# Memory keys and values moved behind the projection units, unit ends cut into steps, the last two units interleaved

## The chip, the cores and the metric

One Trainium2 chip, and one of its cores. The metric is the device time of one launch in microseconds (us); a profiled execution also has a span, from its first instruction to its last. TensorE (PE) multiplies matrices; VectorE (DVE) and ScalarE (ACT) work element by element and empty the accumulators; GpSimd (POOL) does masks and small powers and issues stores; SyncE (SP) issues the loads. Each engine takes its instructions strictly in the order in which they are written for it, so whatever stands behind an instruction that waits, waits too.

## The reference

One layer of a trunk with three parallel mixers, 1024 tokens, width 1024, in float32:

```python
h = rms_norm(x, g_mix[l])
proj = h @ w_in[l]
c_h, c_b, c_c, sq, sk, sv, xq, gate_pre = jnp.split(proj, split_idx, axis=-1)
y_conv = (c_b * causal_depthwise_conv(c_c * c_h, conv_w[l])) @ w_conv_out[l]
o_sb = stick_breaking_attention(to_heads(sq), to_heads(sk), to_heads(sv))
y_sb = o_sb.transpose(0, 2, 1, 3).reshape(b, s, SB_DIM) @ w_sb_out[l]
mem_n = rms_norm(mem, g_mem[l])
y_x = memory_cross_attention(xq, mem_n, w_mem_kv[l], q_norm_g[l], k_norm_g[l]) @ w_x_out[l]
...
merged = gates[:, :, 0] * y_conv + gates[:, :, 1] * y_sb + gates[:, :, 2] * y_x
x = x + merged @ w_out[l]
h2 = rms_norm(x, g_mlp[l])
x = x + jnp.square(jax.nn.relu(h2 @ w_up[l])) @ w_down[l]
```

`mem` has 256 rows; its keys and values are `mem_n @ w_mem_kv` (1024 by 2048), and the keys are normed per head of 256.

## The kernel before

Every float32 operand is split into a high part (ACT casts it to fp32r) and a low part (DVE subtracts), and a product is three matmuls: high by high, high by low, low by high. Stages follow each other:

1. **First stage.** `kv(cg)` makes 256 columns of the memory's keys (`cg` 0 to 3) or values (4 to 7): 2 row tiles of 24 matmuls of 256 columns, in the accumulator `z`. Weights come by `kv_load` (two loads of 512 KB) and are split by `kv_split`. `norm_transpose` turns the normed memory rows into `mem_t`. Keys and values are stored in `kv_scr` and read again later.
   Most of the projections of `h` go through a `Unit`: two blocks of 128 columns for all 1024 tokens by seven products instead of eight (`p1`, `p2`, `p6`, `p5`, `p7`, `p3`, `p4`), each of 12 matmuls of 512 columns; so 84 matmuls a unit. `w1` to `w4` prepare the weights, one `w` for each pair of products, two pairs ahead. `Seconds.first` transposes the first 512 tokens before the first unit; `second_a` and `second_b` make the sums with the other 512 and are called from `hooks` between products. There are 13 units: four for the memory queries (`QUnit`), and three times `HUnit`, `CUnit`, `BUnit` for the convolution. `drive` writes them out pair by pair. `fin` ends a unit; that of a `CUnit` multiplies two tiles, scales each on ACT and adds two shifted copies of each on DVE (`taps`). The calls of `vec`, `act`, `split_o` are pinned to this order (`keep_in_program_order`); the other instructions are put in order by the scheduler.
2. **Heads' values.** `v_steps`: 16 groups of 24 matmuls of 512 columns, which need four weight tiles `us` (split with `unit`, L89 and L90) and `hx`; `h12`, a part of `hx`, is loaded again from `h12_scr` and split first.
3. Cross attention over the memory (`x_scores`, `x_values`), woven with projections; then the stick-breaking attention of 8 pairs of heads, woven with projections (`more`).
4. **Output matrices.** Three times eight blocks (`w_co`, `w_so`, `w_xo`) with the gates, then `w_out` with the residual in `acc`; each finished row tile is normed and stored in `x_scr`.
5. **The wide matrix.** 16 `FUnit`s of the same seven products; `post` and `direct` apply relu and square, `fin` makes sums and stores seven parts in `f_scr`.
6. **The way back.** 28 parts `n` of 48 matmuls (`fetch` loads, `prep` splits), each added to a half of four `acc` tiles on DVE. `acc` is read again from `x_scr` on POOL's queue.

Order in `drive` for the ends and the last pair:

```python
            second()
            if done:
                done.fin()
                done = None
            hook(n, 1)
```

Four buffers of 512 KB (`rawp`) take the loads, three (`whlp`) the split weights, and 40 pages of 512 KB (`pgp`) nearly everything else.

Of the kernel before, what the change touches and what calls it, by code (L numbers as in the profile page):

```python
# [16 lines left out]
P = 128  # L17
# [25 lines left out]
def block_kernel(ctx, tc, x, mem, small, w_in, w_v, w_kv, w_co, w_so, w_xo, w_out, w_up, w_dn, out):  # L43
# [137 lines left out]
    def run(gen):  # L181
        for _ in gen:
            pass

# [149 lines left out]
    class Unit:  # L334
# [86 lines left out]
        def fin(self):  # L421
            pass

    def drive(U, hooks, late=None):

        NU = len(U)
        pairs = [(1, u) for u in range(4)] + [(2, 0), (2, 1), (3, 0), (3, 1)]
        for u in range(2, NU):  # L430
            pairs += [(k, u) for k in ((1, 2, 3) if u >= 4 else (2, 3))]

        def prep(n):
            if n < len(pairs):
                k, u = pairs[n]
                getattr(U[u], f"w{k}")()

        def hook(n, i):
            hooks.get((n, i), lambda: None)()

        for u in range(4):
            U[u].r1 = load(U[u].s1_)
        for n in range(2):
            prep(n)
        hook(-1, 0)
        U[3].bank = po
        done = None
        for n, (k, u) in enumerate(pairs):
            un = U[u]
            first, second = ((un.p1, un.p2), (un.p6, un.p5), (un.p7, un.p3))[k - 1]  # L450
            final = n == len(pairs) - 1
            if final and late:
                late(0)
            first()
            prep(n + 2)
            if n == 1:
                U[0].load()
            if n + 1 < len(pairs) and pairs[n + 1][0] == 3:
                v = pairs[n + 1][1]
                U[v].w4()  # L460
                if v + 2 < NU:
                    U[v + 2].load()
            hook(n, 0)
            if n == 2:
                U[1].load()
            if final and late:
                late(1)
            second()
            if done:
                done.fin()  # L470
                done = None
            hook(n, 1)
            if k == 3:
                if final and late:
                    late(2)
                un.p4()
                done = un
        done.fin()
# [4 lines left out]
    kv_scr = [[dram.tile([P, 1024], F32, name=f"kvscr_{n}_{i}") for i in range(NM)] for n in range(2)]  # L483
# [15 lines left out]
    def kv(cg):  # L499

        us = kv_w.pop(cg)
        to = kn if cg < 4 else vr
        for i in range(NM):
# [10 lines left out]
            nc.scalar.copy(to[i][:, c0 : c0 + 256], ps)  # L514

    def k_norm(i):
# [14 lines left out]
        nc.gpsimd.dma_start(out=kv_scr[0][i], in_=kn[i])  # L531

    mrows = load_rows(mem, 0, NM)
    kv_load(0)
    kv_load(1)
    xrows = load_rows(x, 0, 4)
    mts = [normed(t) for t in mrows]
    mnt = [(page(), page()) for _ in range(2)]
    mem_t = [cut(mnt[k // 4], (k % 4) * M, (k % 4 + 1) * M) for k in range(KT)]
    kv_split(0)  # L540
    run(norm_transpose(mts, lambda k: mem_t[k], C_GMEM))
    kv_split(1)
    kv_load(2)
    kn = [page(F32) for _ in range(NM)]
    run(kv(0))
    rows0 = [normed(t) for t in xrows]
    kv_load(3)
    run(kv(1))
    xrows = load_rows(x, 512, 4)
    kv_split(2)  # L550
    weave(sec_h.first(rows0), kv(2))
    kv_split(3)
    kv_load(4)
    rows1 = [normed(t) for t in xrows]
    run(kv(3))
    for i in range(NM):
        k_norm(i)
    del kn
    vr = [page(F32) for _ in range(NM)]
    kv_split(4)  # L560
    run(kv(4))

    def kv_late(cg):
        kv_split(cg)
        if cg + 1 < 8:
            kv_load(cg + 1)
        run(kv(cg))
        if cg == 7:
            for i in range(NM):
                nc.gpsimd.dma_start(out=kv_scr[1][i], in_=vr[i])  # L570
            pin[0] = False


    class QUnit(Unit):
# [13 lines left out]
    def taps(c, prod, cv, act, stt):  # L588

        act(cv, prod, AF.Copy, scale=tap(c, 2))  # L590
        for j in (1, 2):
            stt(
                out=cv[:, j:1024],
                in0=prod[:, 0 : 1024 - j],
                scalar=tap(c, 2 - j),
                in1=cv[:, j:1024],
                op0=ALU.mult,
                op1=ALU.add,
            )
# [5 lines left out]
    class CUnit(Unit):  # L605
# [6 lines left out]
        def fin(self):  # L612
            self.cv = []
            for i in range(2):
                prod = flat(self.tiles[i])
                vec(prod, prod, ALU.mult, flat(self.hu.tiles[i]))
                cv = flat(self.hu.tiles[i])
                taps(self.c0 + i, prod, cv, act, lambda **kw: order(nc.vector.scalar_tensor_tensor(**kw)))
                self.cv.append(cv)
            self.tiles = self.hu.tiles = None  # L620
# [19 lines left out]
    def a_(kk, cg=None):  # L640
        def go():
            sec_h.second_a(rows1, kk)
            if cg:
                kv_late(cg)

        return go
# [668 lines left out]
```

## Time and profile before

| | us |
|---|---|
| median of 3 runs (2278.94 to 2281.53) | 2281.45 |
| the profiled execution, its own time | 2278.89 |
| its span | 2277.2 |
| PE busy, 10148 instructions | 2180.7 (96%) |
| DVE busy | 1405.6 (62%) |
| ACT busy | 1004.0 (44%) |
| POOL busy | 384.1 (17%) |
| mean granted TensorE clock, share of full | 0.981 |

PE is busy nearly all the time, so the time that is not matmul at full clock is what there is to look for: stretches in which PE is idle, and stretches with a lower granted clock. A view of windows gives both for any stretch: the length, PE's busy time, and the granted clock (`PEclk`). Of two matmuls in a row in the timeline the difference of the starts is the time that one costs; the duration beside it includes pipeline overlap.

### The profile page before, as it was taken

To read this page: it belongs to the slowest core of one execution; us is meant where nothing else is said; L and a number is where in the kernel's file an instruction comes from. 1 tells how busy PE (TensorE), PEld (TensorE's weight loads), DVE (VectorE), ACT (ScalarE), POOL (GpSimd) and SP (SyncE) were. 2 spreads that over 40 slices of the span, in tenths; PEclk is the share of its full clock that TensorE was granted. 3 is DMA by queue.
4 is the path that set the end of the run, shared out by engine and by line. 5 is a ranking of instruction groups with operands and counts; after the bars stand their busy time and mean duration, and the time that the engine had idled before them with its cause. 6 is when DMAs were issued, how large, how long until landed. Compare 5 with 4: busy or idle time off the path is not lost.

```text
span 2277.2 us, 27042 instructions
## 1 busy us (share of the span) xinstructions
PE 2180.7 (96%) x10148; PEld 1804.3 (79%) x10148; DVE 1405.6 (62%) x1885; ACT 1004.0 (44%) x1791; POOL 384.1 (17%) x570
## 2 busy tenths in 40 slices
PE   6799998999999999999999999999989999899999
PEld 6678777888878778778778788888768888688887
DVE  5454555135687788788787534442475555577776
ACT  7333324235566566565566312121465555433332
POOL 1000000112333333433333000000111111100000
PEclk9899999999999999999999999999999999999999
DMA  5332224233222222222222445333234444743443
GB/s 213 120 126 97 71 68 157 86 109 112 77 72 75 84 74 66 83 75 68 81 84 71 137 144 162 107 102 148 105 119 162 152 153 152 257 168 133 153 148 139
DMA packets 76035, 268.13 MB, mean 118 GB/s; under 512 B 9856, under 2 KB 9856, under 8 KB 75904
## 3 DMA queue, kind: packets, MB, share of 16 engines
q1 hardware_dynamic: 54400, 192.47, 26.3%
q0 software_dynamic: 21504, 73.94, 8.6%
q8 instruction: 80, 1.31, 0.2%
q14 instruction: 51, 0.42, 0.1%
HBM read 184.05 MB, written 73.92 MB: 113 GB/s over the span
## 4 chain that ended last, share of the span: by engine, by line
PE 57%; issue 20%; DVE 9%; POOL 7%; ACT 6%; DMA 1%; POOLq 0%; DVEq 0%; ACTq 0%; SPq 0%
PE d L204 5%; PE d L203 5%; PE d L205 5%; PE d L125 4%; PE d L126 4%; PE d L127 4%; PE d L281 4%; PE d L277 4%; PE d L280 4%; POOL pg L866 3%; PE z L281 2%; PE z L277 2%; PE z L280 2%; DVE pg L114 2%; POOL fscr_s L1163 1%
## 5 line engine op out<-in xcount | busy, mean ns | idle before, releaser
L203 PE MATMUL d<-pg,whl 128*128 128x512 f32 x736 | 294.5, 400 | 0.3 <-ACT ox L774 0.3
L236 ACT ACTIVATE pg<-pg 128x512 f32<-128x512 f32 (+1 forms) x192 | 150.7, 790 | 313.2 <-DVE pg L233 311.0
L204 PE MATMUL d<-pg,whl 128*128 128x512 f32 x736 | 287.8, 391 | 0.0
L205 PE MATMUL d<-pg,whl 128*128 128x512 f32 x736 | 287.8, 391 | 0.0
L866 POOL TENSOR_SCALAR_AFFINE_SELECT pg<-pg 128x128 f32<-128x128 f32 x256 | 170.0, 670 | 280.8 <-ACT pg L863 269.7
L876 DVE TENSOR_TENSOR_SCAN pg<-pg,zero 128x128 f32<-128x128 f32 (+7 forms) x128 | 177.0, 1383 | 57.0 <-POOL pg L866 54.2
L233 DVE TENSOR_TENSOR pg<-pg,pg 128x1024 fp32r<-128x1024 f32 (+3 forms) x180 | 183.8, 1031 | 44.8 <-ACT pg L236 42.5
L113 ACT CAST pg<-t 128x256 fp32r<-128x256 f32 (+2 forms) x336 | 115.2, 368 | 203.3 <-DVE pg L114 144.0
L277 PE MATMUL d<-pg,whl 128*128 128x512 f32 x420 | 168.7, 402 | 17.5 <-ACT pg L236 13.8
L280 PE MATMUL d<-pg,whl 128*128 128x512 f32 x420 | 168.0, 400 | 3.3 <-DVE pg L233 3.2
L281 PE MATMUL d<-pg,whl 128*128 128x512 f32 x420 | 167.5, 399 | 1.2 <-DVE whl L233 1.0
L205 PEld LDWEIGHTS d<-pg,whl 128*128 128x128 f32 x736 | 138.1, 188 | 30.7
L203 PEld LDWEIGHTS d<-pg,whl 128*128 128x128 f32 x736 | 138.4, 188 | 25.7 <-ACT ox L774 1.1
L204 PEld LDWEIGHTS d<-pg,whl 128*128 128x128 f32 x736 | 138.6, 188 | 24.3
L277 PE MATMUL z<-pg,whl 128*128 128x512 f32 x396 | 155.9, 394 | 0.0
L280 PE MATMUL z<-pg,whl 128*128 128x512 f32 x396 | 155.2, 392 | 0.0
L281 PE MATMUL z<-pg,whl 128*128 128x512 f32 x396 | 155.0, 391 | 0.0
L125 PE MATMUL d<-pg,whl 128*128 128x512 f32 x384 | 150.6, 392 | 3.2 <-ACT whl L89 3.2
L89 ACT CAST whl<-raw 128x1024 fp32r<-128x1024 f32 x78 | 82.5, 1057 | 159.5 <-DMA raw<-in_w_co 53.1
L126 PE MATMUL d<-pg,whl 128*128 128x512 f32 x384 | 150.3, 392 | 0.0
L233 DVE TENSOR_TENSOR whl<-pg,whl 128x1024 fp32r<-128x1024 f32 x58 | 71.1, 1226 | 127.9 <-ACT whl L236 127.9
L127 PE MATMUL d<-pg,whl 128*128 128x512 f32 x384 | 149.9, 391 | 0.0
(200 smaller groups left out, 4859.0 us busy)
## 6 DMA issues: line engine op xcount, KB each, us to landing
raw<-in_w_in SPq DMA_DIRECT2D x76, 512.0 KB, 3.6
raw<-in_w_up SPq DMA_DIRECT2D x36, 512.0 KB, 3.6
raw<-fscr_s SPq DMA_DIRECT2D x32, 512.0 KB, 3.6
pg<-in_w_dn SPq DMA_DIRECT2D x32, 512.0 KB, 4.9
gscr<-pg POOLq DMA_DIRECT2D x24, 512.0 KB, 2.9
raw<-gscr SPq DMA_DIRECT2D x24, 512.0 KB, 3.7
fscr<-pg POOLq DMA_DIRECT2D x48, 256.0 KB, 2.8
fscr_s<-pg POOLq DMA_DIRECT2D x48, 256.0 KB, 2.8
```

Source lines behind the costliest of these rows:

```text
L125: nc.tensor.matmul(ps, lhsT=ah, rhs=bh, start=i == 0, stop=False)
L126: nc.tensor.matmul(ps, lhsT=ah, rhs=bl, start=False, stop=False)
L127: nc.tensor.matmul(ps, lhsT=al, rhs=bh, start=False, stop=i == n - 1)
L203: nc.tensor.matmul(ps, lhsT=ah, rhs=bh, start=i == 0, stop=False)
L204: nc.tensor.matmul(ps, lhsT=ah, rhs=bl, start=False, stop=False)
L205: nc.tensor.matmul(ps, lhsT=al, rhs=bh, start=False, stop=i == n - 1)
L233: order(nc.vector.tensor_tensor(out=out, in0=a, in1=b, op=op))
L277: m_ = nc.tensor.matmul(ps, lhsT=ah, rhs=bh, start=first and i == 0, stop=False, **go)
L280: nc.tensor.matmul(ps, lhsT=ah, rhs=bl, start=False, stop=False, **go)
L281: nc.tensor.matmul(ps, lhsT=al, rhs=bh, start=False, stop=i == n - 1, **go)
L866: nc.gpsimd.affine_select(out=t_[:, W - P : W], in_=t_[:, W - P : W], pattern=[[-1, P]], compare_op=ALU.is_gt, fill=fill_, base=0, channel ...
L876: nc.vector.tensor_tensor_scan(out=rev, data0=rev, data1=zero.broadcast_to([P, W]), initial=1.0, op0=ALU.mult, op1=ALU.add)
```

## The change

- The memory's keys and values leave the first stage. It now begins with the first 512 tokens' norms and transposes, and the units follow. `mem`'s loads, norms, transposes, the eight `kv(cg)`, and `k_norm` stand in the stage of the heads' values, woven with `v_steps`: each `kv(cg)` with two of its half groups. `kv_scr` is gone; the values are split straight from the accumulator into `vx`.
- `drive` becomes a class `Drive`: `start` loads and splits the first weights, `run` writes the rest. A unit's `fin` is a generator, and one step of the oldest unfinished one is written at each hook. `CUnit.fin` is now four steps: both multiplications, both scalings, then the shifts of one tile and of the other. `FUnit.fin` has two.
- The last two units are written pair by pair side by side, so the last `CUnit` and the last `BUnit`, and the last two `FUnit`s, end together.
- `Drive.start` of the `FUnit`s stands before the last row tiles of `w_out`; `w_co`'s first tile is loaded (`w_first`) before the rest of `more`.
- `acc` is read back in quarters of 128 by 512 for each group of four tiles, two of the four groups before the last `FUnit` products and two after; `block`, `fetch` and `prep` of the first part stand one to four pairs earlier.

```diff
-    def drive(U, hooks, late=None):
...
-        for u in range(2, NU):
-            pairs += [(k, u) for k in ((1, 2, 3) if u >= 4 else (2, 3))]
+    class Drive:
...
+            for u in range(2, NU - 2):
+                self.pairs += [(k, u) for k in ((1, 2, 3) if u >= 4 else (2, 3))]
+            self.pairs += [(k, u) for k in (1, 2, 3) for u in (NU - 2, NU - 1)]
...
+            def hook(n, i):
+                hooks.get((n, i), lambda: None)()
+                if late:
+                    late(n - NP, i)
+                if ends:
+                    if next(ends[0], 0) == 0:
+                        ends.pop(0)
...
+                if k == 3:
+                    un.p4()
+                    ends.append(un.fin())
+            for e in ends:
+                run(e)
...
+            if cg < 4:
+                nc.scalar.copy(kn[i][:, c0 : c0 + 256], ps)
+            else:
+                split(ps, vx[i][0][:, c0 : c0 + 256], vx[i][1][:, c0 : c0 + 256])
...
         def fin(self):
...
+            for i in range(2):
+                vec(prod[i], prod[i], ALU.mult, self.cv[i])
+            yield 1
+            for i in range(2):
+                act(self.cv[i], prod[i], AF.Copy, scale=tap(self.c0 + i, 2))
+            yield 1
+            for i in range(2):
+                for j in (1, 2):
+                    shift(self.c0 + i, j, prod[i], self.cv[i], lambda **kw: order(nc.vector.scalar_tensor_tensor(**kw)))
+                yield 1
...
+    xrows = load_rows(x, 0, 4)
+    dr = Drive(units)
+    rows0 = [normed(t) for t in xrows]
+    dr.start()
+    xrows = load_rows(x, 512, 4)
+    run(sec_h.first(rows0))
+    rows1 = [normed(t) for t in xrows]
+    dr.run(weaving(sec_h, rows1))
...
-    fill(vgen, 17)
+    fill(vgen, 2)
+    mts = [normed(t) for t in load_rows(mem, 0, NM)]
+    kv_load(0)
...
+    for _ in norm_transpose(mts, lambda k: mem_t[k], C_GMEM):
+        fill(vgen, 1)
...
+    for cg in range(8):
+        if cg + 1 < 8:
+            kv_load(cg + 1)
+        if cg == 4:
+            for i in range(NM):
+                k_norm(i)
+            vx[:] = [(page(), page()) for _ in range(NM)]
+        weave(kv(cg), vgen_n(vgen, 2))
+        if cg + 1 < 8:
+            kv_split(cg + 1)
...
+    w_first = unit(w_co[0])
     run(more)
...
+            if ch == 1 and t == 6:
+                df.start()
...
+        elif (n, i) == (-2, 1):
+            prep(0, 0)
+            for t in range(8):
+                acc[t] = page(F32)
+            reload(0, 0)
+        elif (n, i) == (-1, 0):
+            prep(0, 1)
+            reload(4, 1)
...
+    df.run(weaving(sec_f, rows[4:8]), ahead)
+    reload(0, 1)
+    reload(4, 0)
```

PE at the start of the program, before: transposes of the memory rows (tiles `t`) and the keys' matmuls into `z`.

```order
L176 MATMUL t_169<-ident,pg_143 128x128
L176 MATMUL t_174<-ident,pg_143 128x128
L176 MATMUL t_169<-ident,pg_151 128x128
L176 MATMUL t_174<-ident,pg_151 128x128
L203 MATMUL z_222<-whl_162,pg_158 128x256
L204 MATMUL z_222<-whl_162,pg_158 128x256
```

The same place after the change; `pg_127` to `pg_151` are the first four normed row tiles of `x`, `d_279` and `z_297` the first two products of the first unit, `pg_248` a row tile of the other 512 tokens.

```order
L302 MATMUL t_180<-ident,pg_127 128x128
L302 MATMUL t_186<-ident,pg_127 128x128
L302 MATMUL t_180<-ident,pg_135 128x128
...
L284 MATMUL d_279<-pg_192,whl_166 128x512
L287 MATMUL d_279<-pg_193,whl_166 128x512
...
L284 MATMUL z_297<-pg_192,whl_166 128x512
...
L302 MATMUL t_315<-ident,pg_248 128x128
...
L284 MATMUL d_335<-pg_192,whl_168 128x512
```

The units' products have moved to the front; no keys stand before or among them.

DVE at the end of the first stage, before (L618 are the shifts of the last `CUnit`, which stand well before the last products; `pg_2574` and `pg_2521` the last `BUnit`, `raw_2606` the reloaded `h12`, `raw_2672` the first weights of the heads' values).

```order
L618 SCALAR_TENSOR_TENSOR pg_2337<-pg_2453,sm,pg_2337 128x1022
L233 TENSOR_TENSOR pg_2545<-raw_2308,pg_2545 128x512
L233 TENSOR_TENSOR pg_2574<-d_2487,pg_2543 128x512
L233 TENSOR_TENSOR pg_2521<-z_2547,pg_2543 128x512
L233 TENSOR_TENSOR pg_2521<-pg_2521,pg_2281 128x1024
L233 TENSOR_TENSOR pg_2574<-pg_2574,pg_2337 128x1024
L233 TENSOR_TENSOR pg_2615<-raw_2606,pg_2614 128x512 x2
L233 TENSOR_TENSOR pg_2620<-raw_2608,pg_2619 128x512 x2
L90 TENSOR_TENSOR pg_2675<-raw_2672,pg_2674 128x1024
```

And after it (L596 are those shifts, `z_1888` the last product but one, `raw_2060` the first weights of the heads' values):

```order
L240 TENSOR_TENSOR pg_1830<-z_1888,pg_1878 128x512
L596 SCALAR_TENSOR_TENSOR pg_1675<-pg_1794,sm,pg_1675 128x1023
L596 SCALAR_TENSOR_TENSOR pg_1675<-pg_1794,sm,pg_1675 128x1022
L596 SCALAR_TENSOR_TENSOR pg_1729<-pg_1915,sm,pg_1729 128x1023
L596 SCALAR_TENSOR_TENSOR pg_1729<-pg_1915,sm,pg_1729 128x1022
L240 TENSOR_TENSOR pg_1830<-pg_1830,pg_1675 128x1024
L240 TENSOR_TENSOR pg_1958<-pg_1958,pg_1729 128x1024
L240 TENSOR_TENSOR pg_2003<-raw_1998,pg_2002 128x512 x2
L240 TENSOR_TENSOR pg_2008<-raw_2000,pg_2007 128x512 x2
L90 TENSOR_TENSOR pg_2063<-raw_2060,pg_2062 128x1024
```

The four shifts now stand between the last product but one and the first split of the next stage.

DVE where the way back begins, before (`pg_15861`, `pg_15863` are `acc` tiles, `pg_15901` and `pg_15936` the weights' differences for part 1):

```order
L233 TENSOR_TENSOR xh_15858<-pg_15800,pg_15848 128x512
L233 TENSOR_TENSOR pg_15901<-pg_15784,pg_15772 128x1024
L233 TENSOR_TENSOR pg_15904<-pg_15901,pg_15903 128x1024
L233 TENSOR_TENSOR pg_15861<-d_15885,pg_15861 128x512
L233 TENSOR_TENSOR whl_15906<-raw_15780,whl_15906 128x1024
L233 TENSOR_TENSOR pg_15863<-d_15886,pg_15863 128x512
L233 TENSOR_TENSOR pg_15936<-pg_15786,pg_15774 128x1024
```

After (`pg_15800` is the last split of part 0, `z_15686` the last unit's product, `pg_15895` and `pg_15930` the differences for part 1, `pg_15753` an `acc` tile):

```order
L240 TENSOR_TENSOR pg_15800<-raw_15703,pg_15799 128x1024
L240 TENSOR_TENSOR pg_15622<-z_15686,pg_15676 128x512
L240 TENSOR_TENSOR pg_15577<-pg_15577 128x512
L240 TENSOR_TENSOR xh_15833<-pg_15717,pg_15807 128x512
L240 TENSOR_TENSOR pg_15850<-pg_15622,pg_15792 128x512
L240 TENSOR_TENSOR pg_15850<-pg_15850,pg_15622 128x512
L240 TENSOR_TENSOR pg_15622<-pg_15622 128x512
L240 TENSOR_TENSOR xh_15860<-pg_15792,pg_15850 128x512
L240 TENSOR_TENSOR pg_15895<-pg_15727,pg_15645 128x1024
L240 TENSOR_TENSOR pg_15898<-pg_15895,pg_15897 128x1024
L240 TENSOR_TENSOR pg_15753<-d_15879,pg_15753 128x512
L240 TENSOR_TENSOR whl_15900<-raw_15723,whl_15900 128x1024
```

The sums of two units now stand between the splits of part 0 and the differences of part 1; the additions into `acc` keep their place behind these.

More of the change, by code (lines that the diff above doesn't have):

```diff
@@ L183, in run, with vgen_n @@
             pass
+    def vgen_n(gen, n):
+        for _ in range(n):
+            if next(gen, 0) == 0:
+                return
+            yield 1
     def chain(*gens):
@@ new lines, in fin, with __init__, prep, start @@
+            yield 1
+    class Drive:
+        def __init__(self, U):
+            self.U = U
+            NU = len(U)
+            self.pairs = [(1, u) for u in range(4)] + [(2, 0), (2, 1), (3, 0), (3, 1)]
+            for u in range(2, NU - 2):
+                self.pairs += [(k, u) for k in ((1, 2, 3) if u >= 4 else (2, 3))]
+            self.pairs += [(k, u) for k in (1, 2, 3) for u in (NU - 2, NU - 1)]
+        def prep(self, n):
+            if n < len(self.pairs):
+                k, u = self.pairs[n]
+                getattr(self.U[u], f"w{k}")()
+        def start(self):
+            for u in range(4):
+                self.U[u].r1 = load(self.U[u].s1_)
+            for n in range(2):
+                self.prep(n)
+        def run(self, hooks, late=None):
+            U, pairs = self.U, self.pairs
+            NU, NP = len(U), len(pairs)
+            ends = []
+            def hook(n, i):
[5 more added lines that the diff above has]
+                        ends.pop(0)
+            U[3].bank = po
+            for n, (k, u) in enumerate(pairs):
+                un = U[u]
+                first, second = ((un.p1, un.p2), (un.p6, un.p5), (un.p7, un.p3))[k - 1]
+                first()
+                self.prep(n + 2)
+                if n == 1:
+                    U[0].load()
+                if n + 1 < NP and pairs[n + 1][0] == 3:
+                    v = pairs[n + 1][1]
+                    U[v].w4()
+                    if v + 2 < NU:
+                        U[v + 2].load()
+                hook(n, 0)
+                if n == 2:
+                    U[1].load()
+                second()
+                hook(n, 1)
+                if k == 3:
[3 more added lines that the diff above has]
+                run(e)
@@ L530, in k_norm @@
             )
[L531 to L571, printed above, removed]
     class QUnit(Unit):
@@ L1072, in block_kernel @@
             g = load(g_scr[b][d])
-            w = unit(wsrc[d])
+            w = w_first if b + d == 0 else unit(wsrc[d])
             for th in range(2):
@@ L1097, in block_kernel, with __init__, post, direct @@
     }
+    class FUnit(Unit):
+        def __init__(self, u):
+            super().__init__(w_up[u], w_up[16 + u], sec_f)
+            self.u = u
+        def post(self, i, j):
+            t_ = self.dst(i, j)
+            act(t_, t_, AF.Relu)
+            act(t_, t_, AF.Square)
+        def direct(self, a):
+            t_ = self.dst(1, 0)
+            act(t_, a, AF.Relu)
+            act(t_, t_, AF.Square)
+        def fin(self):
+            (fa, fb), fc = self.tiles, pair()
+            self.put("11", fa[:, 0, :])
+            self.put("22", fb[:, 1, :])
+            vec(fc[:, 0, :], fa[:, 1, :], ALU.add, fb[:, 1, :])
+            vec(fc[:, 1, :], fc[:, 0, :], ALU.subtract, fa[:, 0, :])
+            self.put("s1", fc[:, 0, :])
+            yield 1
+            self.put("s2", fc[:, 1, :])
+            vec(fa[:, 1, :], fa[:, 0, :], ALU.subtract, fa[:, 1, :])
+            self.put("s3", fa[:, 1, :])
+            self.put("12", fb[:, 0, :])
+            s4 = self.half()
+            vec(s4, fb[:, 0, :], ALU.subtract, fc[:, 1, :])
+            self.put("s4", s4)
+            yield 1
+        def put(self, n, t_):
+            nc.gpsimd.dma_start(out=f_scr[n, self.u // 4][:, self.u % 4, :], in_=t_)
+    df = Drive([FUnit(u) for u in range(16)])
     for ch in range(2):
```

167 lines of the change are left out of this document (41 added, 126 removed).

## The prediction

> **What bounds it now.** I read the page's busy shares first, then the waits of PE by their releasers, then windows cut where the waits lie.
>
> ```profile
> PE 2180.7 (96%) x10148; PEld 1804.3 (79%) x10148; DVE 1405.6 (62%) x1885; ACT 1004.0 (44%) x1791; POOL 384.1 (17%) x570
> ```
>
> PE is busy for 2180.7 of 2277.2 us, so 96.5 us are waits. They are grouped by what PE waited for (tile and line, releaser: total, times, longest):
>
> ```profile
> PE d L277 <- ACT pg L236: 16.3, 6, 3.6
> ...
> PE z L203 <- ACT whl L89: 11.8, 5, 4.1
> PE z L204 <- DVE whl L90: 9.1, 6, 4.1
> PE t L176 <- DVE st L146: 8.0, 1, 8.0
> PE t L890 <- DVE pg L114: 4.9, 7, 0.7
> PE z L277 <- ACT pg L236: 6.2, 1, 6.2
> PE d L277 <- ACT whl L236: 3.7, 2, 2.3
> PE d L125 <- ACT whl L89: 3.2, 1, 3.2
> ```
>
> The second, third and fourth of the quoted rows (L203 and L204 into `z`, L176) are the memory's keys and values, waiting for their weights' split and for the first norm: 28.9 us. The row of `d` L277 behind `pg` L236 holds the ends of the `CUnit`s, the last two are the starts of the wide matrix and of the output matrices. How long these places are, and at what clock:
>
> ```profile
> core 0: us, PE busy (x) PEld busy (x) DVE busy (x) ACT busy (x) POOL busy (x), PEclk, DMA share, GB/s
> 0.00:67.90 67.90, 45.42 (x296) 42.30 (x296) 31.12 (x56) 41.87 (x79) 9.58 (x20) 0.90 0.55 202
> 67.90:150.00 82.10, 67.27 (x331) 56.75 (x332) 48.12 (x58) 34.43 (x48) 3.26 (x6) 0.88 0.32 109
> 150.00:376.80 226.80, 217.31 (x930) 178.34 (x929) 120.95 (x143) 68.92 (x92) 6.67 (x13) 0.97 0.26 86
> 376.80:389.00 12.20, 8.84 (x29) 6.46 (x28) 8.71 (x10) 7.80 (x11) 0.79 (x2) 0.72 0.79 284
> 400.00:420.00 20.00, 20.00 (x90) 16.58 (x89) 0.00 (x0) 2.35 (x4) 2.85 (x4) 1.00 0.16 48
> 1270.40:1280.00 9.60, 6.35 (x18) 4.95 (x18) 4.58 (x5) 2.24 (x3) 1.80 (x2) 0.64 0.76 259
> 1629.30:1637.20 7.90, 5.46 (x16) 3.75 (x16) 3.32 (x5) 3.04 (x4) 1.13 (x2) 0.79 0.44 148
> 1664.00:1685.00 21.00, 15.05 (x47) 10.00 (x47) 16.24 (x20) 14.06 (x21) 0.90 (x2) 0.76 0.34 100
> 1954.20:1986.00 31.80, 21.63 (x76) 16.52 (x76) 20.01 (x22) 9.66 (x11) 6.96 (x13) 0.84 0.76 276
> ```
>
> The first stage is the first three windows and ends at 376.8. PE idles 22.5 + 14.8 + 9.5 = 46.8 us in it, half of all its waiting. The granted clock falls beside the waits: 0.10 x 67.9 + 0.12 x 82.1 + 0.03 x 226.8 = 23.5 us more. Every wait there is paid nearly one and a half times.
>
> The trace contradicts a rule here. The windows at 1270.4 and 1629.3 hold single waits of 3.2 and 2.3 us and show clocks of 0.64 and 0.79. The Trainium skill (TensorE: Matmul & The Clock Gate, Part 1) says that the clock halves after at least one idle window of about 3.4 us. By that rule these two places would lose no clock, and the gain that I take below for the start of the output matrices and of the wide matrix would be 4.7 us smaller; the measurement decides.
>
> **What the work costs at full clock**, by matmuls in the timeline (start, duration, line): 256 columns wide, two in a row; 512 columns wide, the first and last of twelve.
>
> ```profile
> 20.06 0.28 PE L203 MATMUL z<-pg,pg 128*128 128x256 f32 x1
> 20.18 0.28 PE L204 MATMUL z<-pg,pg 128*128 128x256 f32 x1
> ...
> 371.36 0.39 PE L277 MATMUL z<-pg,whl 128*128 128x512 f32 x1
> ...
> 373.85 0.39 PE L281 MATMUL z<-pg,whl 128*128 128x512 f32 x1
> ```
>
> One costs 0.12 us at 256 columns, and 2.49 / 11 = 0.2264, say 0.2267, at 512. The 8 `kv` groups of 48 are 384 x 0.12 = 46.1 us; the 13 units of 84 are 1092 x 0.2267 = 247.6. With some 9 us of transposes that is 303, and 376.8 - 46.8 - 23.5 = 306.5: the stage is accounted for.
>
> **First stage: -98.9.** It will begin with `x` in place of `mem`. Rows of ACT before: the first row of `mem` is squared at 5.19; a group of transposes of four tokens' tiles is emptied by L296 (two in 1.27) and cast (L113).
>
> ```profile
> 5.19 1.06 ACT L157 ACTIVATE pg<-pg 128x1024 f32<-128x1024 f32 x1 [3.10 <-DMA pg<-in_mem]
> ...
> 28.90 1.27 ACT L296 ACTIVATE pg<-t,sm 128x512 f32<-128x512 f32 x2
> 30.21 1.05 ACT L113 CAST pg<-pg 128x1024 fp32r<-128x1024 f32 x1
> ```
>
> Four row tiles in place of two, each of the size of one of `mem`'s: I take the last as normed at 11.9 (5.19, three further tiles at about 1.3 us, and the norm's tail). Four such groups of 1.27 + about 1.0 on ACT, of which the first product needs three and a part, put it at 20.0. Bounds: 17 (weights ready, ACT free) and 25 (where `x`'s second half and the units' weights share the loads). Then 2.9 at the half clock, 247.6 of products, 3.7 for the 32 transposes of `second_a`, and 3.7 of waiting where `second_b` is due, whose sums stand on DVE between products (the wide matrix has the same sums: window 1664.0, 21.0 - 15.05 = 6 idle and 5 of clock, the upper bound; nothing is the lower one). The ends of `CUnit`s (up to 3.6 each, in the waits) I cost at nothing: in steps, each scaling on ACT stands a hook behind the product that DVE must have made, some 2.7 us of matmuls. Together 277.9, against 376.8. If that cover is too short, up to 3 ends x (3.2 + about 2 of clock) come back.
>
> **Given back among the heads' values: +50.7.** The same 384 x 0.12 and 16 transposes are 47.7; they can't vanish, only move to where nothing waits. The window 400.0 shows that place: PE 20.00 of 20.00, DVE 0.00, ACT 2.35, loads at 48 GB/s. A group needs two casts of 1 us on ACT and two subtractions on DVE, against 5.8 us of its own matmuls and 10.9 of two half groups. I add 3.0 of waits, where the stage begins to need the memory rows and where cross attention starts. Bounds: 0, and the price of the old place, below.
>
> **The end of the first stage: +4.0.** DVE's timeline before, from a shift of the last `CUnit` to the first split of the next stage:
>
> ```profile
> 366.40 1.28 DVE L618 SCALAR_TENSOR_TENSOR pg<-pg,sm,pg 128x1023 f32<-128x1023 f32 x1 [1.27 <-ACT pg L236]
> ...
> 377.64 1.23 DVE L233 TENSOR_TENSOR pg<-pg,pg 128x1024 f32<-128x1024 f32 x1 [1.41 <-ACT pg L236]
> 378.78 2.49 DVE L233 TENSOR_TENSOR pg<-raw,pg 128x512 fp32r<-128x512 f32 x4
> 381.19 2.35 DVE L90 TENSOR_TENSOR pg<-raw,pg 128x1024 fp32r<-128x1024 f32 x2
> ```
>
> The order after puts all four shifts in front of this: 4 x 1.28 = 5.1, of which some 1.1 lies beside the last product. The first low weights (L90) come that much later, and PE, which already idles 3.4 us here, has nothing else. Bounds: 0 (shifts done early) and +9 (5.1 and a further stretch of half clock).
>
> **The start of the output matrices: -6.3.** SP's rows:
>
> ```profile
> 1266.79 0.32 SPq L83 DMA_DIRECT2D raw<-gscr  x1
> 1268.59 0.33 SPq L83 DMA_DIRECT2D raw<-in_w_co  x1
> ```
>
> The weights' load is issued at 1268.6, behind the gates' load, which waited for a buffer; PE waits 3.2 us for their cast. Written earlier, the load takes an earlier buffer, the gates' load the late one, and that is needed only after 24 matmuls. The wait and the clock of the window (0.36 x 9.6 = 3.5, of which I take 3.0) go. Bounds: -7 and 0 (the buffer is late for whichever load comes next).
>
> **The start of the wide matrix: -4.0.** The first weights' casts now stand before the last norms. The window 1629.3 has 2.4 idle and 0.21 x 7.9 = 1.7 of clock. The wait at 1664 stays. Bounds: -4 and 0.
>
> **The start of the way back: -7.5.** The window 1954.2 has 10.2 idle and 0.16 x 31.8 = 5.1 of clock. Its worst wait, 6.2 (`z` L277 behind `pg` L236), follows back to DVE, which stood before an addition into `acc` until it was read back:
>
> ```profile
> 1972.79 0.69 DVE L233 TENSOR_TENSOR pg<-d,pg 128x512 f32<-128x512 f32 x1 [3.80 <-DMA pg<-xscr]
> ```
>
> In quarters, half of them before the last products, `acc` comes in time. What is late next: two units end together, and their sums stand on DVE ahead of part 1's differences. I put half of the old loss there. Bounds: -13 and +2.
>
> **Sum:** -98.9 + 50.7 + 4.0 - 6.3 - 4.0 - 7.5 = -62.0, so a span of 2215.2. The profiled execution took 1.69 us more than its span, and the median of the runs shown lies 2.56 above that: 2219.5.
>
> **Rivals.**
> 1. *The old waits move along.* Loads go out on SP in order, into four buffers, and the pages are nearly all in use in the new place; a group that finds its weights late waits as it did before. The rows of L203 and L204 show 20.9 us in 11 waits for the eight groups. With the longest of both (4.1 + 4.1) and 3.4 of clock for each group, 8 x 11.6 = 93 us, less the 3.0 counted: 2310. It decides from 62 / 8 = 7.8 us a group, and is slower by more than 0.2% (4.6 us, about what a measurement of this kernel can tell) from 8.3. The loads at 48 GB/s and an idle DVE speak against it. Chance 0.03. At a third of that, the new place costs some 30 us: 2247. Chance 0.14.
> 2. *The seams are hidden better.* The first stage starts at 17, `second_b` costs nothing, the shifts run early: 3 + 3.7 + 4 = 10.7 less, 2209. The first stage's windows, with ACT busy 41.87 of 67.9 at its start, speak against it. Chance 0.15.
> 3. *The steps don't do what they say.* A step that is written a hook later still blocks ACT when DVE is behind: the three `CUnit` ends cost 13 again and the way back keeps its 7.5: 2240. DVE's 120.95 of 226.8 leaves it room. Chance 0.1.
>
> That leaves 0.55 for the forecast, with its own range of 2212 to 2232; 0.03 for no difference of over 0.2%, where two of the rivals meet. The range to 2248 takes in the third rival and the middle of the mild first, down to 2207 most of the second. Faster 0.94, same 0.03, slower 0.03.
>
> **What would show it.** In the profile after: the first product of a unit near 20, the last near 278; no idle row for L203 or L204 into `z` of more than 1 us, and DVE and ACT no longer near zero among the heads' values; one wait of about 7 us for L90 at the end of the first stage, larger than before; no wait for the cast of `w_co` and none of 2.3 at the wide matrix's start; one wait of about 5 us in part 1 of the way back, and no addition that waits for `xscr`. Wrong would be a granted clock that falls several times among the heads' values, or waits for weights in the first stage, now that the units' loads come first.

## The result, and the profile after

The changed kernel takes 2228.31 us (median of four runs, 2227.1 to 2230.86) against 2280.25: a ratio of 0.9774, 95% interval 0.9757 to 0.9791. Forecast were 2219.5 us and 2207 to 2248. The direction and the range held; of the forecast gain of 62 us, 52 came. The profiled execution after is the slowest of its four runs (2230.86, span 2229.2), and the one before (2278.89) is faster than all four of its own, so the two traces differ by 48.0 us only. The sums below go by the traces.

The waits of PE after, grouped as before (tile and line, releaser: total, times, longest; L284 is the line that was L277, L210 to L212 those that were L203 to L205):

```profile
PE t L302 <- DVE st L146: 9.6, 4, 7.5
PE d L284 <- ACT pg L243: 7.3, 2, 3.7
...
PE d L211 <- DVE pg L90: 4.4, 1, 4.4
PE d L210 <- ACT pg L89: 3.7, 1, 3.7
PE d L287 <- DVE pg L240: 3.4, 6, 0.8
PE z L284 <- ACT pg L243: 2.6, 1, 2.6
```

The keys' and values' rows into `z`, 20.9 us before, are gone; nothing of them has taken a place among the waits. The wait for the first norm (8.0 at L176 before) isn't gone: it stands at L302 now, longest 7.5, for `x` in place of `mem`. The wait for `w_co` (3.2) and that of 2.3 at the wide matrix's start are gone. What has grown stands at the end of the first stage: 3.7 for L89 and 4.4 for L90, where 2.8 and 0.5 stood before. In all PE idles 64.8 us, 96.5 before.

Stage by stage, cut at the first product or matmul of each stage; first the kernel before, then the changed one:

```profile
core 0: us, PE busy (x) PEld busy (x) DVE busy (x) ACT busy (x) POOL busy (x), PEclk, DMA share, GB/s
0.00:67.92 67.92, 45.42 (x296) 42.30 (x297) 31.14 (x56) 41.88 (x79) 9.58 (x20) 0.90 0.55 202
67.92:376.81 308.89, 284.59 (x1261) 235.08 (x1262) 169.06 (x200) 103.33 (x140) 9.94 (x19) 0.94 0.28 92
376.81:476.92 100.11, 96.75 (x429) 79.53 (x428) 24.89 (x27) 30.76 (x45) 14.79 (x19) 0.97 0.41 137
476.92:1273.74 796.82, 772.96 (x3878) 642.15 (x3878) 599.37 (x901) 465.94 (x1066) 274.94 (x376) 1.00 0.25 80
1273.74:1631.67 357.93, 355.61 (x1574) 293.77 (x1574) 142.79 (x179) 76.34 (x92) 10.00 (x18) 0.99 0.39 131
1631.67:1954.28 322.61, 316.52 (x1376) 258.30 (x1376) 200.37 (x267) 176.16 (x259) 57.91 (x107) 0.98 0.45 153
1954.28:2277.20 322.92, 308.85 (x1339) 253.20 (x1338) 238.02 (x258) 109.62 (x113) 6.96 (x13) 0.98 0.47 161
```

```profile
core 0: us, PE busy (x) PEld busy (x) DVE busy (x) ACT busy (x) POOL busy (x), PEclk, DMA share, GB/s
0.00:19.33 19.33, 8.31 (x32) 5.91 (x33) 7.06 (x14) 14.74 (x21) 2.91 (x10) 1.00 0.89 351
19.33:288.05 268.72, 258.86 (x1126) 210.38 (x1124) 161.22 (x200) 100.75 (x138) 10.93 (x20) 0.98 0.26 85
288.05:439.88 151.83, 143.74 (x815) 125.39 (x814) 52.28 (x72) 56.16 (x100) 15.68 (x22) 0.97 0.40 136
439.88:1239.35 799.47, 777.85 (x3891) 645.75 (x3890) 599.90 (x901) 466.65 (x1067) 274.02 (x376) 1.00 0.25 81
1239.35:1593.20 353.85, 353.22 (x1571) 291.57 (x1570) 144.85 (x181) 78.92 (x94) 10.25 (x16) 1.00 0.41 134
1593.20:1925.39 332.19, 326.04 (x1431) 266.36 (x1429) 212.12 (x281) 181.65 (x266) 67.82 (x126) 0.99 0.48 164
1925.39:2229.20 303.81, 296.44 (x1291) 243.67 (x1290) 227.63 (x247) 104.00 (x106) 2.15 (x4) 0.99 0.45 154
```

| stage | forecast | measured |
|---|---|---|
| first stage (376.81 to 288.05) | -98.9 | -88.8 |
| heads' values with keys and values, and the seam ahead (100.11 to 151.83) | +54.7 | +51.7 |
| cross attention and stick-breaking, to the first `w_co` matmul (796.82 to 799.47) | -3.3 | +2.7 |
| output matrices, to the first wide product (357.93 to 353.85) | -5.3 | -4.1 |
| wide matrix and way back (645.53 to 636.00) | -9.2 | -9.5 |
| sum | -62.0 | -48.0 |

The two starts lie on cuts between stages: of the 6.3 for `w_co` the wait (3.3) counts in the stage ahead and the clock (3.0) in the one behind, and of the 4.0 for the wide matrix 2.3 and 1.7.

Where the terms are, in the changed kernel's windows: the place of `second_b`, the seam, the stage that took the keys, the start of cross attention, and the start of the way back.

```profile
62.80:75.00 12.20, 6.93 (x17) 4.40 (x17) 9.81 (x13) 5.88 (x9) 0.00 (x0) 0.72 0.27 87
...
288.05:303.50 15.45, 7.36 (x19) 5.37 (x19) 12.64 (x13) 7.60 (x10) 1.06 (x2) 0.67 0.61 224
303.50:440.00 136.50, 136.50 (x797) 120.14 (x796) 39.77 (x60) 48.68 (x91) 14.62 (x20) 1.00 0.38 125
440.00:455.00 15.00, 13.82 (x81) 12.37 (x82) 8.86 (x18) 5.62 (x12) 4.03 (x2) 0.89 0.31 106
...
1921.00:1945.00 24.00, 20.59 (x77) 15.76 (x76) 19.50 (x22) 10.91 (x12) 3.81 (x8) 0.86 0.72 264
```

The row from 303.50 to 440.00 is the point of the change: in these 136.5 us, with the keys and values in them, PE is busy 136.50 at full clock, while DVE is busy 39.77 and ACT 48.68. Two places lose more than the forecast gave them: `second_b` 12.20 - 6.93 = 5.3 idle and 0.28 x 12.2 = 3.4 of clock, 8.7 in place of 3.7; the seam 8.1 idle and 0.33 x 15.45 = 5.1, 13.2 in place of 10.8 (6.8 + 4.0).

Idle time and clock can't always be added, since half clock costs nothing while PE waits. At the seam 0.33 x 15.45 means 10.2 us at half clock, but matmuls start 0.43 us apart, in place of 0.23, only from 297.3 to 303.0. A count of matmuls has no such overlap: 17 of them, 3.9 us at 0.2267, take 15.25 us (288.05 to 303.30), so 11.4 are lost. Before, 16 of them (3.6) and eight transposes (about 0.8) took 11.28 (376.81 to 388.09), so 6.9 were lost. By this count the seam grew by 4.5 us. At `second_b`, where little waiting falls into the half clock, the count of matmuls gives 8.4.

The seam's queue on DVE (the four shifts, two products with B, the splits of `h12`, the first weights' low parts) stands as the order showed it:

```profile
286.29 5.11 DVE L596 SCALAR_TENSOR_TENSOR pg<-pg,sm,pg 128x1023 f32<-128x1023 f32 x4
291.31 2.35 DVE L240 TENSOR_TENSOR pg<-pg,pg 128x1024 f32<-128x1024 f32 x2
293.58 2.49 DVE L240 TENSOR_TENSOR pg<-raw,pg 128x512 fp32r<-128x512 f32 x4
295.99 2.35 DVE L90 TENSOR_TENSOR pg<-raw,pg 128x1024 fp32r<-128x1024 f32 x2
```

### The profile page after: what moved, and what is told of

Its sections match the earlier page's. It is cut to its first block, busy times and chain, and to the rows that moved or that the text cites. A ratio compares the mean times of both kernels' runs of the same rounds, so it can differ in the third digit from the quotient of the medians.

```text
span 2229.2 us, 27032 instructions
## 1 busy us (share of the span) xinstructions
PE 2164.5 (97%) x10148; PEld 1789.0 (80%) x10148; DVE 1405.1 (63%) x1891; ACT 1002.9 (45%) x1789; POOL 383.8 (17%) x574
## 4 chain that ended last, share of the span: by engine, by line
PE 72%; DVE 11%; issue 7%; ACT 6%; POOL 4%; DMA 1%; POOLq 0%; ACTq 0%; DVEq 0%; SPq 0%
PE d L211 6%; PE d L212 6%; PE d L210 6%; PE d L287 6%; PE d L288 6%; PE d L284 6%; PE d L126 4%; PE d L127 4%; PE d L125 4%; PE z L288 4%; PE z L284 4%; PE z L287 4%; DVE pg L240 3%; POOL pg L847 2%; DVE pg L114 2%
## 5 line engine op out<-in xcount | busy, mean ns | idle before, releaser
L210 PE MATMUL d<-pg,whl 128*128 128x512 f32 x736 | 294.6, 400 | 0.1
L212 PE MATMUL d<-pg,whl 128*128 128x512 f32 x736 | 288.1, 391 | 0.0
L284 PE MATMUL d<-pg,whl 128*128 128x512 f32 x420 | 166.3, 396 | 7.3 <-ACT pg L243 7.3
L212 PEld LDWEIGHTS d<-pg,whl 128*128 128x128 f32 x736 | 138.3, 188 | 30.7
L210 PEld LDWEIGHTS d<-pg,whl 128*128 128x128 f32 x736 | 138.4, 188 | 25.2 <-ACT ox L755 0.5
L284 PE MATMUL z<-pg,whl 128*128 128x512 f32 x396 | 156.0, 394 | 0.0
L90 DVE TENSOR_TENSOR whl<-raw,whl 128x1024 fp32r<-128x1024 f32 x78 | 99.1, 1271 | 83.1 <-ACT whl L89 82.4
L89 ACT CAST whl<-raw 128x1024 fp32r<-128x1024 f32 x78 | 82.5, 1058 | 152.8 <-DMA raw<-in_w_co 47.9
```

The source lines that it names most:

```text
L210: nc.tensor.matmul(ps, lhsT=ah, rhs=bh, start=i == 0, stop=False)
L212: nc.tensor.matmul(ps, lhsT=al, rhs=bh, start=False, stop=i == n - 1)
L284: m_ = nc.tensor.matmul(ps, lhsT=ah, rhs=bh, start=first and i == 0, stop=False, **go)
```

## Experiments

Each kernel was timed in five rounds beside the kernel before. The changed kernel itself came along as the measure. Differences to it go by ratios: a ratio is uncertain by 0.0013 to 0.0015, so two differ clearly from about 0.002, or 4.5 us.

### The changed kernel again

> The changed kernel itself, as the common measure for the experiments: 2228 us (2225 to 2231). If the granted clock drops after short waits at other places than in the first profile, with the same waits, then the length of the half-clock stretches is partly chance.

2229.25 us, ratio 0.9783 (0.9770 to 0.9797). The trace has the same waits in the same places, among them 3.69 at 64.3 and 1.18 at 441.8, and yet a span of 2225.2. The last section shows what differs.

### Keys and values alone

Everything else as before: `fin` in one piece, units one after another, old starts, old reload.

```diff
-            for u in range(2, NU - 2):
+            for u in range(2, NU):
...
-            self.pairs += [(k, u) for k in (1, 2, 3) for u in (NU - 2, NU - 1)]
...
-    w_first = unit(w_co[0])
...
-            if ch == 1 and t == 6:
-                df.start()
...
```

> Only the memory's keys and values are moved; unit ends in one piece two products later, the last units one after another, w_co's and the wide matrix's first weights and the residual as before. Theory (the move is plain work put where nothing waits, and gives most of the gain; the other parts repair single waits): 2228 + 13 (three ends of CUnits at 3.2 us and about a half-clock window each, less the 2 us left now) - 6 (end of the first stage) + 7 (start of the output matrices) + 4 (wide matrix) + 8 (way back) = 2254, so 26 us faster than before, with no wait of over 1 us for the keys' weights and sums of second_b that hold PE for about 8 us. Rival (the gain comes from the steps and starts, the move only moves its waits): 2270 to 2280, with waits among the heads' values.

2256.5 us, ratio 0.9905 (0.9891 to 0.9918): 22 us faster than before. The time is that of the theory; its words "most of the gain" are not right, since 22 of the 52 us come from the move alone. Among the heads' values no wait is left here either (window 320 to 440). PE's rows where `second_b` is due, and then the window around them:

```profile
68.45 0.79 PE L284 MATMUL d<-pg,whl 128*128 128x512 f32 x1 [3.69 <-ACT pg L243]
69.98 0.79 PE L287 MATMUL d<-pg,whl 128*128 128x512 f32 x1 [0.74 <-DVE pg L240]
```

```profile
62.80:75.00 12.20, 6.92 (x16) 4.20 (x16) 10.27 (x14) 5.91 (x9) 0.00 (x0) 0.60 0.26 87
320.00:440.00 120.00, 120.00 (x720) 106.69 (x719) 34.58 (x49) 40.61 (x75) 11.37 (x15) 1.00 0.36 117
```

In the kernel before, the same place had waits of 0.64, 1.03 and 0.46. With the keys' work away, 5.3 us of waiting and a half clock of 0.40 x 12.2 = 4.9 stand there; by the matmuls 8.8 us are lost, since part of the half clock falls into the wait. The keys' work had been a cover for the sums of `second_b`. DVE shows it: two splits of weights ahead of these sums, in the kernel before and then here.

```profile
129.64 1.23 DVE L233 TENSOR_TENSOR whl<-pg,whl 128x1024 fp32r<-128x1024 f32 x1 [4.57 <-ACT whl L236]
135.08 1.23 DVE L233 TENSOR_TENSOR whl<-pg,whl 128x1024 fp32r<-128x1024 f32 x1 [2.40 <-ACT whl L236]
```

```profile
55.33 1.22 DVE L240 TENSOR_TENSOR whl<-pg,whl 128x1024 fp32r<-128x1024 f32 x1 [1.19 <-ACT whl L243]
59.86 1.23 DVE L240 TENSOR_TENSOR whl<-pg,whl 128x1024 fp32r<-128x1024 f32 x1 [1.50 <-ACT whl L243]
```

Before, the last 48 keys' matmuls (256 columns) stand on PE from 114.9 to 125.1, and DVE is so far ahead of PE by the first split that it idled 4.57 us, behind ACT, which waited 2.37 for a product of PE. Here no such matmuls stand there, DVE idled 1.19, ACT waited 3.91 for DVE, and PE arrives at the sums before they are made. At this term the forecast of the first stage was off. (The start of the stage, with `x` ahead, differs between the two kernels as well; it was not tried apart.)

### The end of a `CUnit` in one piece

```diff
+            yield 1
             for i in range(2):
                 vec(prod[i], prod[i], ALU.mult, self.cv[i])
-            yield 1
-            for i in range(2):
                 act(self.cv[i], prod[i], AF.Copy, scale=tap(self.c0 + i, 2))
-            yield 1
-            for i in range(2):
                 for j in (1, 2):
                     shift(...)
-                yield 1
```

> Only CUnit.fin is put back in one piece, two products after the unit. Theory (the scaling on ACT, written right behind DVE's product, blocks ACT and so PE): waits of about 3.2 us again at the two inner CUnits, each with a half-clock window of 1.7 us, in place of 0.97: +6 to +10, 2234 to 2238. Rival (without the keys' work on ACT and DVE the ends are hidden in any form): 2228, waits stay under 1 us.

2243.85 us, ratio 0.9844 (0.9831 to 0.9858): 14 us slower than the changed kernel, more than expected. The two inner ends cost 3.16 us each again, as the theory said. The rest is the last `CUnit`, whose end falls into the seam; ACT there:

```profile
295.60 1.15 ACT L243 ACTIVATE pg<-pg,sm 128x1024 f32<-128x1024 f32 x1 [6.70 <-DVE pg L240]
300.62 1.15 ACT L243 ACTIVATE pg<-pg,sm 128x1024 f32<-128x1024 f32 x1 [3.87 <-DVE pg L240]
...
304.23 1.98 ACT L89 CAST pg<-raw 128x1024 fp32r<-128x1024 f32 x2
```

Each scaling waits for DVE's product, DVE makes two shifts of the first tile before the second product, and the next stage's first cast stands behind it all: PE's wait for L89 is 8.9 us in place of 3.7.

### The last two units one after another

```diff
-        def __init__(self, U):
+        def __init__(self, U, tail=2):
...
-    dr = Drive(units)
+    dr = Drive(units, 0)
```

The new argument of `Drive` is the number of units at the end that are written side by side.

> The first stage's last two units stand one after another again, the wide matrix's stay side by side. Theory (the four shifts of the last CUnit stand on DVE before the next stage's first low weights, because both units end together): the wait for L90 falls from 4.4 us to under 1, the wait for L89 to about 3, and the half-clock stretch shortens from 10 to 7 us: -6, 2222. Rival (the loads of the next stage's weights or the splits of h12 set it): within 2 us of 2228, with the same two waits.

2226.31 us, ratio 0.9769 (0.9755 to 0.9782): 3 us less than the changed kernel, which the intervals do not separate from it. The trace does what the theory said: the wait for L90, 4.1 and 4.4 us in the two traces of the changed kernel, falls to 0.83, and that for L89 stays 3.69. The window of the seam (16 us, PE busy 11.47, clock 0.89) loses 4.5 + 1.8:

```profile
288.00:304.00 16.00, 11.47 (x43) 8.45 (x42) 10.01 (x12) 10.37 (x15) 2.36 (x4) 0.89 0.85 325
```

That is 6.9 less than the changed kernel's 13.2 there; by the count of matmuls 6.6 are lost in place of 11.4, so 4.8 less, where 6 were expected. 3 of them show in the medians. So these runs show no gain from writing the last two units side by side in this stage.

### The old starts

```diff
-    w_first = unit(w_co[0])
...
-            w = w_first if b + d == 0 else unit(wsrc[d])
+            w = unit(wsrc[d])
```

and `df.start()` after the last row tile.

> w_first is taken out and the wide matrix's first weights are loaded after the last row tile's norm, as before. Theory: the waits of 3.25 and 2.30 us come back, each with its half-clock stretch (3.4 and 1.7 us): +10.6, 2239. Rival (the clock falls only after an idle window of about 3.4 us, so these waits cost themselves alone): +5.5, 2234. Second rival (w_co's load was late for another reason and only another load is late now): +4, 2232.

2239.46 us, ratio 0.9822 (0.9808 to 0.9835): 9 us more by the ratios, 10 by the medians. Waits of 3.53 and 2.30 us are back, each with a half clock, in these windows:

```profile
1239.00:1250.00 11.00, 7.47 (x26) 5.46 (x25) 5.29 (x6) 2.50 (x4) 1.80 (x2) 0.84 0.73 241
1597.00:1608.00 11.00, 8.56 (x33) 6.14 (x32) 3.87 (x5) 4.14 (x6) 1.13 (x2) 0.84 0.42 144
```

The waits and 0.16 x 11 of clock in each make 5.8 + 3.5 = 9.3. Both rivals gave less; the time alone, uncertain by some 4 us, would not rule out the first of them, but the clock in the two windows does, above all after the wait of 2.30.

### The old start of the way back

```diff
-            for t in range(8):
-                acc[t] = page(F32)
-            reload(0, 0)
...
-            reload(4, 1)
...
-    reload(0, 1)
-    reload(4, 0)
+    for t in range(8):
+        acc[t] = page(F32)
+        nc.gpsimd.dma_start(out=acc[t], in_=x_scr[t])
```

and `block`, `fetch` and `prep` of part 0 at the last pair.

> block, fetch and prep of part 0 and the reload of acc stand as before (whole tiles on POOL's queue after the last unit); the last two FUnits stay side by side. Theory (additions that wait for acc hold DVE, and with it part 1's splits): idle 10 us in place of 3.4 at the start of the way back, and a second half-clock stretch: +8, 2236, with additions behind xscr again. Rival (the side-by-side ends alone are what helped): +2, 2230.

2243.2 us, ratio 0.9839 (0.9826 to 0.9853): 13 us more, where 8 were expected. The addition into `acc` that stands before the splits of part 1 now waits longer than in the kernel before (8.29 against 2.95 and 3.80):

```profile
1934.70 0.69 DVE L240 TENSOR_TENSOR pg<-d,pg 128x512 f32<-128x512 f32 x1 [8.29 <-DMA pg<-xscr]
```

From 1908 to 1945 PE idles 37.0 - 25.23 = 11.8 us here, with 0.22 x 37 = 8.1 of clock; in the changed kernel it is 3.4 and 0.09 x 37 = 3.3. In the kernel before, this place had 10.2 and 5.1, so it is worse than it was. POOL issues the first loads of `acc` at 1923.75, right behind the last store of the two units, and the last ones at 1933.29. That the two ends together make it worse was not tried apart. The early reload and the early splits, which the next run parts, make the place pay.

### The old reload alone

```diff
-            for t in range(8):
-                acc[t] = page(F32)
-            reload(0, 0)
...
-            reload(4, 1)
...
-    reload(0, 1)
-    reload(4, 0)
+    for t in range(8):
+        acc[t] = page(F32)
+        nc.gpsimd.dma_start(out=acc[t], in_=x_scr[t])
```

with `block`, `fetch` and `prep` of part 0 early, as in the changed kernel.

> Only the reload of acc stands as before: whole tiles on POOL's queue after the last unit; block, fetch and prep of part 0 stay early. It parts the old start of the way back (+13) in two. Theory (the addition that waits for acc holds DVE): an addition behind xscr waits 5 us or more, and the kernel takes 2238 to 2242. Rival (the late loads and splits of part 0 were most of it): 2229 to 2233, with no such wait of over 2 us.

2236.38 us, ratio 0.9814 (0.9800 to 0.9827): 7 us more than the changed kernel, so about half of the 13, and just below the theory's range. The addition waits, and PE behind it for 6.47 us in part 1:

```profile
1926.25 0.69 DVE L240 TENSOR_TENSOR pg<-d,pg 128x512 f32<-128x512 f32 x1 [6.38 <-DMA pg<-xscr]
```

The other 6 us are left for the late loads and splits of part 0; with them late as well, PE has waits of 0.89, 2.62 and 1.55 us between 1913 and 1921, which are missing here. Quarters and an earlier place came together here; quarters alone were not tried.

### The seam: what is left of the ends, later

```diff
-            for e in ends:
-                run(e)
+            self.ends = ends
...
     fill(vgen, 2)
+    for e in dr.ends:
+        run(e)
...
```

> Not part of the change: what is left of the last two units' ends (shifts and products with B in the first stage) is written after the first two steps of the heads' values, so DVE splits the next weights first; in the wide matrix nothing moves. Theory: the wait for L90 (4.4 us) and part of the half-clock stretch go, the first wait of 3.7 for ACT stays or shrinks: -5 to -8, 2221 to 2223. Rival (the splits of h12 or the loads set it): 0.

2223.58 us, ratio 0.9757 (0.9742 to 0.9771): 6 us less than the changed kernel, as expected. The wait for L90 is down to 0.20, that of 3.7 for L89 stays, with one short stretch at half clock:

```profile
287.00:303.00 16.00, 11.73 (x44) 8.45 (x43) 11.88 (x12) 10.35 (x14) 0.74 (x1) 0.89 0.72 255
```

### `second_b` three products earlier

```diff
-        hooks.update({(4 + kk // 2, kk % 2): b_(sec, kk) for kk in range(4)})
+        hooks.update({at: b_(sec, kk) for kk, at in enumerate(((2, 1), (3, 0), (3, 1), (4, 0)))})
```

> Not part of the change: the four hooks of second_b stand three products earlier, in the first stage and in the wide matrix. Theory (the last sum is written one product before p7 needs it, while DVE and ACT had waited 3.7 us for each other shortly before): the stall of 5.2 us idle and 3.4 of clock in the first stage, and of 5.1 and 3.4 in the wide matrix, falls by half or more: -8 to -15, 2213 to 2220. Rival (DVE is full from the first product on, so the stall is only moved to an earlier product): within 3 us of 2228, with a wait of the same size two products earlier.

2225.17 us, ratio 0.9759 (0.9746 to 0.9773): 5 us less by the ratios. The time is above the theory's range and inside the rival's (within 3 us of 2228), but the trace shows one of them in each stage. In the first, three waits of 0.76, 1.00 and 1.28 us (and two of 0.53) take the place of 0.76, 3.69 and 0.74, and the clock stays whole. In the wide matrix the rival holds: the 3.6 us for the sums become waits of 3.5 and 2.4 for the split weights (`whl`). The row of these waits over the whole trace, with the 0.76 and 1.00 of the first stage in it:

```profile
PE d L284 <- ACT whl L243: 7.7, 4, 3.5
```

### Three combinations

All three have the ends later, and the reload and splits of `h12` behind `fill(vgen, 2)` too; they differ in the hooks of `second_b`. In `best_a` it stands three products earlier in the first stage only; in `best_b` two earlier there and one in the wide matrix, and the first queries of cross attention are split before the keys' transposes; in `best_c` two earlier in both.

> Not part of the change: what is left of the last units' ends, and also the reload and the splits of h12, are written after the first two steps of the heads' values; second_b stands three products earlier in the first stage only. Theory (the seam between the stages is set by what stands on ACT and DVE ahead of the next weights' splits, and by nothing else): both waits of the seam (3.7 and 4.1 to 4.4 us) and its half-clock stretch (5) go, 13 in all, and the first stage ends 4 earlier as with the earlier hooks alone: 2212. Rival (the next weights can't be loaded and split that early, since buffers are held): the seam keeps one wait of about 4 us and its half clock, 2218 to 2220.

2216.68 us, ratio 0.9727 (0.9713 to 0.9740). The seam is whole: PE is busy 15.00 of 15.00 us around it, with no wait left in this window. That is the theory; the time lies 5 above the 2212 that it gave and 1 below the rival's 2218 to 2220, so it is the trace and not the time that tells them apart.

```profile
284.00:299.00 15.00, 15.00 (x67) 12.42 (x67) 12.94 (x14) 8.91 (x15) 2.48 (x3) 1.00 0.91 325
```

> As best_a, but second_b two products earlier in the first stage and one in the wide matrix, and the first queries of cross attention are split before the keys' transposes. Theory: the wait of 1.2 us for POOL and its half-clock stretch go (-1.2 to -4.6), and the wide matrix's stall of 5.1 us and 3.4 of clock halves (-4): 2205 to 2208. Rival (in the wide matrix ACT is full, with relu and square, so that any earlier place only moves the stall to the split weights): 2211 to 2213.

2215.3 us, ratio 0.9717 (0.9704 to 0.9730), the best of all: 15 us less than the changed kernel, 65 less than the one before. The wait for POOL at cross attention is gone. In the wide matrix a wait of 1.71 for split weights and one of 3.14 for the sums stand where 3.62 and two of 0.75 stood: the rival, though the time is a little above the rival's 2211 to 2213 too.

> As best_a, but second_b two products earlier in both stages. Theory: in the wide matrix two products are between the old place (one wait of 3.6 for the sums) and three (waits of 3.5 and 2.4 for split weights); if ACT's order sets it, the stall is least here, -5 in the wide matrix: 2207. Rival (ACT is full there): the idle time stays at 5 to 6 us in other places, 2212.

2216.27 us, ratio 0.9722 (0.9709 to 0.9736). Waits of 3.42 (split weights) and 1.97 (sums) in the wide matrix: the rival again, with the time 4 above its 2212. The three are the same within their intervals, and the times by the theories were 5 to 10 us too low. That an earlier place of the hooks shifts the stall in the wide matrix and doesn't remove it is shown for three places; that ACT's relu and square are what fills it was argued only.

## Why the prediction was right, and where it was off

- *What bounds, and the move.* Right. Half of PE's waiting (46.8 of 96.5 us) lay in the first stage, and the 20.9 us for the keys' and values' weights are gone after the move; the first norm's wait only changed from `mem` to `x`. The returned work costs 151.83 - 11.4 = 140.4, against 100.11 - 6.9 = 93.2 before: 47.2. Another 1.7 belong to it: sixteen matmuls of one column (`t` L699, once L718) stood ahead of the cut before and stand behind it now. Together 48.9, where 47.7 and 3.0 of waits were forecast. The full clock and the 136.50 of 136.50 show that DVE and ACT had the room that the window at 400 promised. The first rival (the waits move along), priced from 30 to 90 us, didn't happen.
- *First stage, -98.9.* The mis-sized term is "3.7 of waiting where `second_b` is due": it measures 8.7, and the kernel with the move alone shows why, as told above. The forecast had the right row beside it, the wide matrix's window at 1664 with 6 and 5, and called it the upper bound; it is the same code without keys ahead of the products, and so the nearest row rather than a bound. The start came at 19.33 (20.0 forecast). Two ends of `CUnit`s keep 0.97 each, which were costed at nothing. Between 26 and 38, where `second_a` waits for the second half's norms, 12.0 - 10.22 = 1.8 idle and 0.14 x 12 = 1.7 of clock weren't in the sum at all. Together 5.0 + 1.9 + 3.5 - 0.7 = 9.7. Against this stands the term "2.9 at the half clock", for which the prediction gives no row: in this trace the first twelve matmuls from 19.33 on start 0.23 us apart, at full clock, but for a first step of 0.56 and one wait of 0.73. So 1.1 were lost there, and the term is 1.8 too large. Of the missing 10.1 us, 7.9 have a place, then, and 2.2 have none here.
- *The seam, +4.0.* The mechanism was right. By the windows the size was 6.4 (13.2 against 6.8), by the count of matmuls 4.5. The count has no overlap in it, so the term was nearly right. The shifts took 5.11 as forecast, and 1.8 of that lies beside the last product (286.29 to 288.05), where 1.1 was forecast. The sign that was named for it came otherwise: not one wait of 7 for L90, but 3.7 for L89 and 4.4 for L90.
- *Cross attention.* The stretch up to the first `w_co` matmul is 2.7 longer and not 3.3 shorter. The wait for `w_co` is gone, as forecast. Against its 3.3 stand the sixteen matmuls that changed sides of the cut (1.7), a wait of 1.18 for POOL at 442 with half clock after it (0.11 x 15 = 1.7), and half clock again near 500 (1.7): 6.3 in all, so 3.0 where 2.7 were measured. Waits of this kind were forecast among the heads' values, "where cross attention starts", and came here.
- *The three starts.* `w_co`, the wide matrix and the way back gave about what was forecast: their windows lose 0, 0 and 3.4 + 3.4 now. The prediction set a rule of the Trainium skill (TensorE: Matmul & The Clock Gate, Part 1) against the trace, and 4.7 us hung on it. Taking the two starts back brings 5.8 of waits and 3.5 of clock, so the trace's reading held. Only the wait of 2.30 tells against the rule's idle window of about 3.4 us, with 1.7 of clock; the other was 3.53.
- *Rivals.* Of the three conditions of the second (hidden seams) none came true in the change as it is. The combined kernels come down to 2215 to 2217, still above its 2209: their seam is whole, but `second_b` still waits in them. Of the third (ends that still block), nothing is left but the 0.97 twice.

## What to carry to other kernels

Work that is taken out of a stage takes a cover with it: look in the trace for a later stage that has the same code without that work, and price the bare place by that row. What ends a stage should not be written ahead of what the next one needs first, on any engine: writing the next stage's first splits ahead of the units' ends alone was worth 6 us here, about as much as the early reload. Ends that come together need their followers (a reload, a split) written before them: without these, the changed kernel was 13 us slower. And add idle time and lost clock only where they don't overlap.

## What the runs showed of the hardware

The half clock is partly chance. Two executions of the changed kernel, with the same waits; the windows at 26 (waits of 0.5 and 1.04 us), 440 (one of 1.18) and 496 (the first execution's longest is 0.51); first one execution, then the other:

```profile
26.00:38.00 12.00, 10.22 (x47) 7.76 (x46) 9.73 (x14) 6.41 (x10) 2.27 (x4) 0.86 0.37 123
440.00:452.00 12.00, 10.82 (x61) 9.59 (x62) 7.19 (x12) 4.42 (x8) 4.03 (x2) 0.86 0.25 89
496.00:508.00 12.00, 11.49 (x63) 9.78 (x62) 4.91 (x9) 4.74 (x8) 2.79 (x3) 0.86 0.62 201
```

```profile
26.00:38.00 12.00, 10.17 (x54) 7.58 (x53) 9.73 (x14) 6.42 (x10) 2.37 (x4) 1.00 0.36 123
440.00:452.00 12.00, 10.82 (x62) 9.45 (x61) 6.83 (x13) 3.77 (x7) 4.04 (x2) 0.86 0.28 91
496.00:508.00 12.00, 11.70 (x71) 10.19 (x70) 5.95 (x13) 5.25 (x11) 2.75 (x3) 1.00 0.62 197
```

A lost 0.14 x 12 = 1.7 us is one stretch of 3.4 us at half speed: in the first execution matmuls start 0.43 us apart, in place of 0.23, from 29.9 to 33.3. It followed waits of about 1 us in one execution and not in the other, and the spans differ by 4.0 us. The second execution in turn starts its first products 0.43 us apart (20.0 to 22.2), and the first does not. So waits far below 3.4 us can cost clock. The other windows above lose about two or three times as much (0.28 x 12.2 = 3.4, 0.33 x 15.45 = 5.1), so in these traces the clock that a place loses is 0 or close to a multiple of 1.7 us, less what PE waits in it. A term of this kind in a sum is uncertain by that much however well the wait is known.
